# Gate and up projection from seven block products instead of eight, with the down projection as a stage of its own

## The chip, the cores and the metric

The kernel runs on one core of a Trainium2 chip. The metric is the device time of one execution in microseconds (us): the median of three runs of the kernel before is 2223.04 us (2222.63 to 2224.3). All tensors are float32; every product is made of float32r passes.

## The reference, cut to what matters

The reference is one layer of a streaming encoder on 512 tokens of width 2048: an input projection, three groups of mixing heads (attention, convolution, spatial gating), an output projection with residual, and a gated feed forward of width 5632. The change touches the feed forward and what lies around it:

```python
x = x + jnp.einsum('bse,ed->bsd', y, w_out[l])
h = rms_norm(x, ffn_norm[l])
gate = causal_depthwise_conv(jnp.einsum('bsd,df->bsf', h, w_gate[l]), ffn_conv_w[l], ffn_conv_b[l])
up = jnp.einsum('bsd,df->bsf', h, w_up[l])
x = x + jnp.einsum('bsf,fd->bsd', jax.nn.silu(gate) * up, w_down[l])
return rms_norm(x, final_norm)
```

Here h is 512 x 2048, w_gate and w_up are 2048 x 5632, the depthwise convolution has three taps along the tokens, and w_down is 5632 x 2048.

## The kernel before

The names P, S, KT, NT and NF stand for 128 partitions, 512 tokens, 16 tiles of 128 along the width, 4 token tiles and 44 tiles of 128 along the feed-forward width.

Every product is taken three times, in `mm3` (line 291): each operand is split into a part rounded to float32r and the exact rest, and hi*hi, hi*lo and lo*hi are added up in one PSUM bank. `split` (line 255) makes the two parts: ScalarE copies the operand to float32r (`w_hi`), and then VectorE subtracts that copy from the operand (`w_lo`). Both inputs of the subtraction lie in SBUF. The norm of the residual stream is applied after the product, as a scale of each token (`row2`).

The weights come in chunks of 512 KB through three buffers (`w_load`, line 246), in the order of one list, `plan`. `w_split` (line 262) splits half a chunk, that is 128 x 512 elements, and issues the next load. The matmul loops use half a chunk at a time and issue the split of the half chunk that comes two later (`w_ahead`, line 287), so that ScalarE and VectorE work ahead of TensorE.

`proj_t` (line 296) makes 256 columns of a projection, transposed: two PSUM banks of 128 columns x 512 tokens, each from 16 x 3 matmuls with a weight tile of 128 x 128 as the stationary and 512 tokens as the moving operand. `proj_n` (line 315), used earlier for other columns, makes its products with the activations as the stationary and 256 columns of weights as the moving operand; the trace names its banks `pn`.

After the output projection (lines 866 to 879) the residual stream stays in 16 SBUF tiles. Lines 880 to 883 turn it into the transposed and split operand `hT2` of the feed forward: 64 transposes on TensorE, 16 activations on ScalarE and 16 operations on VectorE (`load_transposed`, line 400). The feed forward (lines 910 to 941) runs over 11 groups of 512 columns. A group has four products of 256 columns: gate, up, gate, up. After a gate product, VectorE scales its banks, ScalarE applies the last tap and the bias, VectorE adds the two other taps, and ScalarE applies silu. After an up product, VectorE scales the bank, GpSimd multiplies it with the gate (`ff_t`), and the result is split and kept in SBUF. One column block of the down projection of the group before (`down`, line 897, banks `pd`) follows each product; VectorE adds its four banks to the residual tiles. The last group's down projection is taken token tile by token tile together with the final norm (lines 943 to 975, banks `pl`).

Each engine takes its instructions in the order in which they are issued, and the order is written out by hand: the splits of later weights stand between the matmuls of the present ones. Before the feed forward a planner (`Issue`) sets side work between the projections; in the feed forward none is left.

## Time and profile before

| What | Value |
|---|---|
| median of 3 runs | 2223.04 us (2222.63 to 2224.3) |
| the profiled execution: its span, from first to last instruction | 2222.3 us, 0.7 us less than that median |
| TensorE busy | 2188.3 us, 98% |
| VectorE busy | 1171.5 us, 53% |
| ScalarE busy | 844.5 us, 38% |
| GpSimd busy | 222.3 us, 10% |
| mean DMA rate | 96 GB/s |

The profile shows one execution. PE is TensorE, PEld its weight load, DVE is VectorE, ACT is ScalarE, POOL is GpSimd, SP is the engine that issues the DMAs (SPq is its queue). L105 is the line through which all three of ScalarE, VectorE and GpSimd are called, and L168 that of all matmuls, so that the tile names tell the groups apart: `pt` banks of a transposed projection, `pn` of a natural one, `po` of the output projection, `pd` and `pl` of the down projection. In a row of the timeline stand the start, the time from there to the end of the last merged instruction, the engine, the line, the operation, the tile written and those read, the shapes and the count; in brackets the idle time of the engine before it and what ended it. In a group of instructions stand the busy time, the mean duration of one in ns, and the idle time before them. In a table by stretch each engine's busy time and count is followed by the granted clock of TensorE (1.00 is 2.4 GHz, 0.50 is 1.2 GHz), the share of time for which the DMA engines were busy, and the rate. Matmuls are pipelined: the distance between two starts, not the duration, tells what one costs in a stream.

### The profile page before, as it was taken

How to read it: one execution, taken by the hardware profiler on the slowest of the kernel's cores; microseconds unless marked ns; L12 is line 12 of the kernel's file. 1: busy time of each engine (PE TensorE's matmuls, PEld its weight loads, DVE VectorE, ACT ScalarE, POOL GpSimd, SP SyncE). 2: the span in 40 equal slices, each digit the busy share in tenths (PEclk: the TensorE clock that was granted, in tenths of full speed). 3: DMA queues.
4: the chain of work that ended last, by engine and by line, in shares of the span. 5: the costliest groups of instructions: out<-in, count | busy, mean ns of one | idle time of the engine just before them, and what ended most of it. 6: DMA issues, size and time to landing. Idle time of an engine off the chain costs nothing.

```text
span 2222.3 us, 26797 instructions
## 1 busy us (share of the span) xinstructions
PE 2188.3 (98%) x10361; PEld 1831.2 (82%) x10361; DVE 1171.5 (53%) x1828; ACT 844.5 (38%) x1516; POOL 222.3 (10%) x295
## 2 busy tenths in 40 slices
PE   8999999999999999999999999999999999999998
PEld 7888888898788888888888888888888888888886
DVE  4789897986733444444444344344334434434446
ACT  5335567767632423222222222232222223222233
POOL 2012232322200000000000000000000000000002
PEclk9999999999999999999999999999999999999999
DMA  5332222222243232332332333233233333323343
GB/s 179 95 93 79 67 68 66 67 62 67 76 142 121 88 96 95 105 95 86 107 102 87 103 95 97 93 105 95 85 112 97 92 98 97 99 89 104 95 131 106
DMA packets 176559, 213.20 MB, mean 96 GB/s; under 512 B 6981, under 2 KB 138929, under 8 KB 176433
## 3 DMA queue, kind: packets, MB, share of 16 engines
q1 hardware_dynamic: 175873, 211.23, 30.6%
q8 instruction: 81, 1.33, 0.2%
q14 instruction: 45, 0.37, 0.1%
q10 hardware_dynamic: 560, 0.27, 0.0%
HBM read 207.28 MB, written 4.19 MB: 95 GB/s over the span
## 4 chain that ended last, share of the span: by engine, by line
PE 89%; DVE 6%; ACT 2%; issue 1%; POOL 1%; DMA 0%; SPq 0%; ACTq 0%; POOLq 0%; DVEq 0%
PE pt L168 53%; PE pd L168 20%; PE po L168 8%; PE pn L168 3%; PE pl L168 2%; DVE cv_acc L105 1%; DVE w_lo L105 1%; ACT e L105 1%; PE av L168 1%; PE ps_tr L172 1%; PE z_C L168 1%; PE z_A L168 1%; PE z_B L168 0%; DVE wt_lo L105 0%; POOL newton L105 0%
## 5 line engine op out<-in xcount | busy, mean ns | idle before, releaser
L105 DVE TENSOR_TENSOR w_lo<-w_raw,w_hi 128x512 fp32r<-128x512 f32 x752 | 521.3, 705 | 765.4 <-ACT w_hi L105 765.1
L105 ACT CAST w_hi<-w_raw 128x512 fp32r<-128x512 f32 x752 | 456.6, 621 | 928.4 <-PE pt L168 681.8
L168 PE MATMUL pt<-hT_hi,w_hi 128*128 128x512 f32 x1856 | 723.4, 390 | 0.1
L168 PE MATMUL pt<-hT_hi,w_lo 128*128 128x512 f32 x1856 | 723.2, 390 | 0.3 <-DVE w_lo L105 0.3
L168 PE MATMUL pt<-hT_lo,w_hi 128*128 128x512 f32 x1856 | 723.1, 390 | 0.0
L168 PEld LDWEIGHTS pt<-hT_hi,w_lo 128*128 128x128 f32 x1856 | 348.5, 188 | 73.8 <-DVE w_lo L105 1.2
L168 PEld LDWEIGHTS pt<-hT_hi,w_hi 128*128 128x128 f32 x1856 | 348.6, 188 | 71.3 <-ACT w_hi L105 0.8
L168 PEld LDWEIGHTS pt<-hT_lo,w_hi 128*128 128x128 f32 x1856 | 348.6, 188 | 70.2
L168 PE MATMUL pd<-w_hi,t_hi 128*128 128x512 f32 x640 | 249.0, 389 | 0.0
L168 PE MATMUL pd<-w_lo,t_hi 128*128 128x512 f32 x640 | 249.0, 389 | 0.0
L168 PE MATMUL pd<-w_hi,t_lo 128*128 128x512 f32 x640 | 249.0, 389 | 0.0
L105 POOL TENSOR_TENSOR ff_t<-ff_t,ff_c 128x512 f32<-128x512 f32 x44 | 56.8, 1290 | 1316.9 <-DVE ff_t L105 1316.9
L168 PEld LDWEIGHTS pd<-w_lo,t_hi 128*128 128x128 f32 x640 | 120.1, 188 | 25.0
L168 PEld LDWEIGHTS pd<-w_hi,t_lo 128*128 128x128 f32 x640 | 120.1, 188 | 24.9
L168 PEld LDWEIGHTS pd<-w_hi,t_hi 128*128 128x128 f32 x640 | 120.1, 188 | 24.9
L168 PE MATMUL pn<-w_hi,hT_hi 128*128 128x256 f32 x384 | 108.6, 283 | 0.0
L168 PE MATMUL pn<-w_hi,hT_lo 128*128 128x256 f32 x384 | 108.5, 283 | 0.0
L168 PE MATMUL pn<-w_lo,hT_hi 128*128 128x256 f32 x384 | 108.5, 282 | 0.0
L168 PE MATMUL po<-w_hi,yT_hi 128*128 128x512 f32 x256 | 100.5, 393 | 2.6 <-DVE sg_u L105 2.6
L168 PE MATMUL po<-w_lo,yT_hi 128*128 128x512 f32 x256 | 100.2, 391 | 0.0
L168 PE MATMUL po<-w_hi,yT_lo 128*128 128x512 f32 x256 | 100.1, 391 | 0.0
L105 DVE TENSOR_TENSOR x<-x,pd 128x512 f32<-128x512 f32 x160 | 98.9, 680 | 0.0
(212 smaller groups left out, 1998.4 us busy)
## 6 DMA issues: line engine op xcount, KB each, us to landing
w_raw<-in_w_gate_dram SPq DMA_DIRECT2D x88, 512.0 KB
w_raw<-in_w_up_dram SPq DMA_DIRECT2D x88, 512.0 KB
w_raw<-in_w_down_dram SPq DMA_DIRECT2D x88, 512.0 KB
w_raw<-in_w_in_dram SPq DMA_DIRECT2D x80, 512.0 KB
w_raw<-in_w_out_dram SPq DMA_DIRECT2D x32, 512.0 KB
x<-in_x_dram SPq DMA_DIRECT2D x32, 256.0 KB
out_dram<-x SPq DMA_DIRECT2D x16, 256.0 KB
gain<-in_final_norm_dram SPq DMA_DIRECT2D x4, 256.0 KB
```

What stands on the lines that cost most here:

```text
L105: ins = f(*a, **k)
L168: return nc.tensor.matmul(o, lhsT=lhsT, rhs=rhs, start=start, stop=stop, skip_group_check=True)
L172: nc.tensor.transpose(out=o, in_=in_, identity=identity)
```

## The change

The mathematics of gate and up changes. The 2048 rows of the weights are taken as two halves, the 256 columns of a product as two halves of 128, and the 512 tokens as two halves of 256. The eight block products of this 2 x 2 x 2 scheme are replaced by seven products of sums of blocks. On the side of the activations the seven operands (`R11`, `R21`, `R22`, `T1` to `T4`) are made once, for each of the eight pairs of width tiles, and split. On the side of the weights, four of the seven operands (`S1` to `S4`) are sums of blocks that GpSimd makes anew for each product; all seven are split as before. A product of 256 columns then has 14 units (7 block products, each in two halves of four width tiles) of 12 matmuls, with a weight tile of 128 x 128 as the stationary and 256 tokens as the moving operand. The four quarters of the result are added up by VectorE from four half banks.

The down projection is taken out of the loop over gate and up. The gated result of each tile of 128 columns is stored to a tensor in HBM (`t_dram`), and the residual stream as well (`x1_dram`); a stage behind the last product loads both again. This stage takes the down projection in four runs over ten tiles each, with all four column blocks, and the last four tiles token tile by token tile as before. SBUF is cut into pools that belong to stages: a pool of a later stage takes the room of an earlier one, tile by tile as these come free.

The diff, cut to its core:

```diff
+    groups = [(w, 256 * fp) for fp in range(NF // 2) for w in (w_gate, w_up)]
+    def blk_load(g):
+        if g < len(groups):
+            src, c0 = groups[g]
+            for h in range(2):
+                for q in range(2):
+                    t = raw_pool.tile([P, 4, 256], F32, tag="raw", bufs=6, name="b_raw")
+                    k0 = (8 * h + 4 * q) * P
+                    nc.sync.dma_start(
+                        out=t, in_=src[k0 : k0 + 4 * P, c0 : c0 + 256].rearrange("(k p) c -> p k c", p=P)
+                    )
+                    blk[g, h, q] = t
...
             add2(tt, nb, x1[nb][tt])
-    hT2 = []
+            nc.sync.dma_start(out=x1_dram[nb][tt], in_=x1[nb][tt])
+        if nb == 3:
+            blk_load(0)
...
     with tc.issue_after(end.ins):
-        for nb in range(4):
-            hT2 += load_transposed(x1[nb], nb, mm if nb % 2 == 0 else zz, 32)
+        for j in range(8):
+            fa, fb, ta, tb = (tmp(n) for n in ("f_a", "f_b", "t_a", "t_b"))
+            for kt, f in ((j, fa), (j + 8, fb)):
+                ps = zz("ps_tr")
+                for tt in range(NT):
+                    transpose(
+                        ps[:, tt * P : (tt + 1) * P], x1[kt // 4][tt][:, (kt % 4) * P : (kt % 4 + 1) * P], ident
+                    )
+                act_.activation(f, ps, AF.Copy, scale=gcol(32 + kt))
+            hi = ap.tile([P, 7, HT], F32R, name=f"R_hi{j}")
+            lo = ap.tile([P, 7, HT], F32R, name=f"R_lo{j}")
+            r11, r12, r21, r22 = fa[:, 0:HT], fa[:, HT:S], fb[:, 0:HT], fb[:, HT:S]
+            split(hi[:, 0, :], lo[:, 0, :], r11)
+            vec.tensor_tensor(out=ta[:, 0:HT], in0=r12, in1=r11, op=ALU.subtract)
+            pool.tensor_tensor(out=tb[:, 0:HT], in0=r22, in1=r12, op=ALU.subtract)
+            vec.tensor_tensor(out=ta[:, HT:S], in0=r22, in1=ta[:, 0:HT], op=ALU.subtract)
+            pool.tensor_tensor(out=tb[:, HT:S], in0=r21, in1=ta[:, HT:S], op=ALU.subtract)
+            for at, src in ((5, fb), (1, ta), (3, tb)):
+                split(
+                    hi[:, at : at + 2, :], lo[:, at : at + 2, :], src.rearrange("p (n t) -> p n t", n=2)
+                )
+            Rm.append((hi, lo))
...
+    SEQ = (
+        ("L11", "R11"), ("S1", "T1"), ("L12", "R21"), ("S3", "T3"), ("S2", "T2"), ("S4", "R22"), ("L22", "T4"),
+    )
+    UNITS = [(g, i, q) for g in range(len(groups)) for i in range(7) for q in range(2)]
+    SUMS = {
+        "S1": ("L21", "L22", ALU.add), "S3": ("L11", "L21", ALU.subtract),
+        "S2": ("S1", "L11", ALU.subtract), "S4": ("L12", "S2", ALU.subtract),
+    }
+    def make_sum(n):
...
+        if name in SUMS:
+            a, b, op = SUMS[name]
+            t = sp.tile([P, 4, P], F32, tag="sum", bufs=6, name="b_sum")
+            pool.tensor_tensor(out=t, in0=operand(g, a, q), in1=operand(g, b, q), op=op)
+            sums[g, name, q] = t
+    def make_split(n):
...
+        if i == 0 and q == 0:
+            blk_load(g + 1)
+        hi = sp.tile([P, 4, P], F32R, tag="bhi", bufs=5, name="b_hi")
+        lo = sp.tile([P, 4, P], F32R, tag="blo", bufs=5, name="b_lo")
+        split(hi, lo, operand(g, SEQ[i][0], q))
+        parts[n] = (hi, lo)
...
+    def gate_out(f, c):
+        vec.tensor_tensor(out=c, in0=c, in1=row2, op=ALU.mult)
+        s = tmp("ff_c")
+        act_.activation(s, c, AF.Identity, bias=fcol(3, f), scale=fcol(2, f))
+        for k in (1, 0):
+            sh = 2 - k
+            vec.scalar_tensor_tensor(
+                out=s[:, sh:S], in0=c[:, 0 : S - sh], scalar=fcol(k, f), in1=s[:, sh:S],
+                op0=ALU.mult, op1=ALU.add,
+            )
+        act_.activation(s, s, AF.Silu)
+        pool.tensor_tensor(out=s, in0=s, in1=row2, op=ALU.mult)
+        sil[f] = s
+    def up_out(f, c):
+        pool.tensor_tensor(out=c, in0=c, in1=sil.pop(f), op=ALU.mult)
+        nc.sync.dma_start(out=t_dram[f], in_=c)
+    AHEAD, SUM_AHEAD = 4, 6
...
+        b1, b2 = mm("pt"), mm("pt")
+        X, Y, Z1, Z2 = b1[:, 0:HT], b1[:, HT:S], b2[:, 0:HT], b2[:, HT:S]
+        acc = {0: X, 1: Z1, 2: Y, 3: Z2, 4: X, 5: Z1, 6: Z2}
+        c0, c1 = tmp("ff_g0"), tmp("ff_g1")
+        for i in range(7):
+            for q in range(2):
+                make_sum(n + SUM_AHEAD)
+                make_split(n + AHEAD)
+                hi, lo = parts.pop(n)
+                at = R_AT[SEQ[i][1]]
+                for kk in range(4):
+                    rh, rl = Rm[4 * q + kk]
+                    mm3(
+                        acc[i], hi[:, kk, :], lo[:, kk, :], rh[:, at, :], rl[:, at, :],
+                        i < 2 and q == 0 and kk == 0, q == 1 and kk == 3,
+                    )
+                n += 1
+            if i == 2:
+                vec.tensor_copy(c0[:, 0:HT], X)
+                vec.tensor_tensor(out=c0[:, 0:HT], in0=c0[:, 0:HT], in1=Y, op=ALU.add)
+            elif i == 3:
+                vec.tensor_copy(c1[:, HT:S], Z1)
+                vec.tensor_tensor(out=c1[:, HT:S], in0=c1[:, HT:S], in1=Z2, op=ALU.add)
+            elif i == 4:
+                u = tmp("ff_u")[:, 0:HT]
+                act_.copy(u, X)
+                vec.tensor_tensor(out=c1[:, HT:S], in0=c1[:, HT:S], in1=u, op=ALU.add)
+            elif i == 5:
+                vec.tensor_tensor(out=c0[:, HT:S], in0=u, in1=Z1, op=ALU.add)
+                out_fn(f0, c0)
+            elif i == 6:
+                vec.tensor_tensor(out=c1[:, 0:HT], in0=u, in1=Z2, op=ALU.add)
+                out_fn(f0 + 1, c1)
...
+    for f in range(4):
+        t_load(f)
+        dn_load(f)
+    t_next = 0
+    for _ in range(4):
+        t_split(t_next)
+        t_next += 1
+    for j in range(3):
+        dn_split(j)
...
+    for kg in range(4):
+        for nb in range(4):
+            banks = [(mm if nb % 2 else zz)("pd") for _ in range(NT)]
+            if kg == 0:
+                for tt in range(NT):
+                    nc.sync.dma_start(out=x1[nb][tt], in_=x1_dram[nb][tt])
+            for f in range(10 * kg, 10 * kg + 10):
+                if t_next < min(NF, 10 * kg + 24) and (t_next < 10 * kg + 10 or j % 2 == 0):
+                    t_split(t_next)
+                    t_next += 1
...
+                for tt in range(NT):
+                    ts_ = slice(tt * P, (tt + 1) * P)
+                    th, tl = t_parts[f]
+                    mm3(banks[tt], th[:, ts_], tl[:, ts_], hi, lo, f == 10 * kg, f == 10 * kg + 9)
+            for tt in range(NT):
+                vec.tensor_tensor(out=x1[nb][tt], in0=x1[nb][tt], in1=banks[tt], op=ALU.add)
```

`raw_block` takes 128 of the 256 columns of a loaded chunk, and `operand` takes such a block or a sum. `t_split` and `dn_split` split a tile of the gated result and half a chunk of `w_down`.

## Rows read from the trace of the kernel before

**Rows 1.** The page: busy time of each engine.
```profile
PE 2188.3 (98%) x10361; PEld 1831.2 (82%) x10361; DVE 1171.5 (53%) x1828; ACT 844.5 (38%) x1516; POOL 222.3 (10%) x295
```
**Rows 2.** The chain of waits in order: start us, us, what.
```profile
928.52 21.76 PE pt L168 x96
950.28 10.88 PE pd L168 x48
```
**Rows 3.** Timeline of TensorE: first and nineteenth matmul of a stretch of `proj_n`.
```profile
111.76 0.28 PE L168 MATMUL pn<-w_hi,hT_hi 128*128 128x256 f32 x1
...
113.92 0.28 PE L168 MATMUL pn<-w_hi,hT_hi 128*128 128x256 f32 x1
```
**Rows 4.** Groups of instructions by form in the feed forward, 790 to 2165 us.
```profile
L105 DVE TENSOR_TENSOR w_lo<-w_raw,w_hi 128x512 fp32r<-128x512 f32 x508 | 342.9, 690 | 615.3 <-ACT w_hi L105 615.3
L105 DVE SCALAR_TENSOR_TENSOR ff_c<-ff_g,cols_f,ff_c 128x511 f32<-128x511 f32 x44 | 33.1, 751 | 38.0 <-ACT ff_c L105 38.0
L105 ACT CAST w_hi<-w_raw 128x512 fp32r<-128x512 f32 x507 | 306.4, 622 | 709.5 <-PE pt L168 596.6 <-PE pd L168 110.8 <-DMA w_raw<-in_w_down_dram 2.2
L105 ACT ACTIVATE ff_c<-ff_g,cols_f 128x512 f32<-128x512 f32 x44 | 35.6, 808 | 52.1 <-DVE ff_g L105 52.1
L105 ACT ACTIVATE ff_c<-ff_c 128x512 f32<-128x512 f32 x44 | 27.8, 633 | 71.6 <-DVE ff_c L105 71.6
L105 POOL TENSOR_TENSOR ff_t<-ff_t,ff_c 128x512 f32<-128x512 f32 x44 | 56.8, 1290 | 1316.9 <-DVE ff_t L105 1316.9
```
**Rows 5.** Timeline of VectorE: two `w_lo` without GpSimd, at 779 us.
```profile
779.53 1.28 DVE L105 TENSOR_TENSOR w_lo<-w_raw,w_hi 128x512 fp32r<-128x512 f32 x2
```
**Rows 6.** Timeline of VectorE beside GpSimd, 113 to 121 us.
```profile
117.44 3.48 DVE L105 TENSOR_TENSOR w_lo<-w_raw,w_hi 128x512 fp32r<-128x512 f32 x2
120.85 0.73 DVE L105 SCALAR_TENSOR_TENSOR cv_acc<-cv_a,cols_c,cv_acc 128x507 f32<-128x507 f32 x1
```
**Rows 7.** Timeline of GpSimd in the same stretch.
```profile
115.23 3.44 POOL L105 TENSOR_TENSOR cv_a<-cv_a,cv_g 128x512 f32<-128x512 f32 x2
118.64 1.74 POOL L105 TENSOR_TENSOR cv_acc<-cv_acc,cv_sq 128x512 f32<-128x512 f32 x1
```
**Rows 8.** Timeline of VectorE beside GpSimd, with an operand in PSUM.
```profile
366.29 1.27 DVE L105 TENSOR_TENSOR k_f<-pt,row_x 128x512 f32<-128x512 f32 x2
367.49 0.67 DVE L105 TENSOR_TENSOR w_lo<-w_raw,w_hi 128x512 fp32r<-128x512 f32 x1
```
**Rows 9.** Timeline of GpSimd in that stretch.
```profile
365.87 1.66 POOL L105 TENSOR_TENSOR sq<-sq,newton 128x512 f32<-128x512 f32 x1
```
**Rows 10.** Groups by form: 256 columns on VectorE and on ScalarE.
```profile
L105 DVE TENSOR_TENSOR v<-vf,v 128x256 fp32r<-128x256 f32 x16 | 6.7, 419 | 1.9 <-ACT v L105 1.8
L105 ACT CAST v<-vf 128x256 fp32r<-128x256 f32 x16 | 6.5, 407 | 0.5
```
**Rows 11.** Timeline of TensorE and ScalarE between output projection and feed forward.
```profile
765.25 8.74 PE L172 MATMUL ps_tr<-ident,x 128*128 128x128 f32 x64
774.00 0.50 PE L168 MATMUL pt<-hT_hi,w_hi 128*128 128x512 f32 x1
...
767.22 9.35 ACT L105 ACTIVATE hT_hi<-ps_tr,cols_a 128x512 fp32r<-128x512 f32 x16
```
**Rows 12.** Table by stretch: the first 20 us, and around 450 us.
```profile
0.00:10.00 10.00, 4.30 (x16) 3.34 (x17) 1.45 (x3) 3.06 (x4) 4.37 (x22) 1.00 0.76 244
10.00:20.00 10.00, 9.75 (x46) 7.88 (x46) 7.04 (x11) 8.97 (x22) 0.73 (x4) 1.00 0.95 336
445.00:449.80 4.80, 3.15 (x14) 2.02 (x13) 4.73 (x7) 0.60 (x1) 2.72 (x4) 1.00 0.30 91
449.80:453.30 3.50, 3.50 (x13) 2.94 (x13) 2.81 (x5) 2.38 (x5) 0.00 (x0) 0.51 0.09 29
```
**Rows 13.** Timeline of TensorE at the lower clock, 591 to 593 us.
```profile
590.88 0.63 PE L168 MATMUL po<-w_hi,yT_lo 128*128 128x512 f32 x1
...
592.58 0.63 PE L168 MATMUL po<-w_hi,yT_hi 128*128 128x512 f32 x1
```

More of the change, by code (lines that the diff above doesn't have):

```diff
@@ L944, in trunk_kernel @@
-    gain = [s2k("gain") for _ in range(4)]
+    t_dram = [dram.tile([P, S], F32, name=f"t_{f}") for f in range(NF)]
+    sil = {}
+    def gate_out(f, c):
[11 more added lines that the diff above has]
+        sil[f] = s
@@ new lines, in up_out @@
+    def up_out(f, c):
+        pool.tensor_tensor(out=c, in0=c, in1=sil.pop(f), op=ALU.mult)
+        nc.sync.dma_start(out=t_dram[f], in_=c)
+    AHEAD, SUM_AHEAD = 4, 6
+    for n in range(SUM_AHEAD):
+        make_sum(n)
+        if n < AHEAD:
+            make_split(n)
+    n = 0
+    for g in range(len(groups)):
+        f0 = 2 * (g // 2)
+        out_fn = gate_out if g % 2 == 0 else up_out
+        b1, b2 = mm("pt"), mm("pt")
[31 more added lines that the diff above has]
+                out_fn(f0 + 1, c1)
@@ new lines, in trunk_kernel, with dn_load @@
+    a_stage.close()
+    up_stage.close()
+    d_stage = ctx.enter_context(ExitStack())
+    dp = d_stage.enter_context(tc.tile_pool(name="down", bufs=1, reuse_waits="tile"))
+    dplan = [(f, nb) for kg in range(4) for nb in range(4) for f in range(10 * kg, 10 * kg + 10, 2)]
+    dplan += [(f, nb) for nb in range(4) for f in (40, 42)]
+    n_steps = 2 * 16 * 5
+    raw_d, halves_d, t_parts = {}, {}, {}
+    def dn_load(i):
+        if i < len(dplan):
+            f, nb = dplan[i]
+            raw_d[i] = dp.tile([P, 2, S], F32, tag="raw", bufs=4, name="w_raw")
+            nc.sync.dma_start(
+                out=raw_d[i],
+                in_=w_down[f * P : (f + 2) * P, nb * S : (nb + 1) * S].rearrange("(k p) c -> p k c", p=P),
+            )
@@ new lines, in big, with dn_split @@
+    def big(name):
+        return dp.tile([P, S], F32R, tag="big", bufs=52, name=name)
+    def dn_split(j):
+        i, s = divmod(j, 2)
+        if i >= len(dplan):
+            return
+        if j < n_steps:
+            hi = dp.tile([P, S], F32R, tag="whi", bufs=4, name="w_hi")
+            lo = dp.tile([P, S], F32R, tag="wlo", bufs=4, name="w_lo")
+        else:
+            hi, lo = big("w_hi"), big("w_lo")
+        split(hi, lo, raw_d[i][:, s, :])
+        halves_d[j] = (hi, lo)
+        if s == 1:
+            del raw_d[i]
+            dn_load(i + 4)
@@ new lines, in trunk_kernel, with t_load, t_split @@
+    t_raw = {}
+    def t_load(f):
+        if f < NF:
+            t_raw[f] = dp.tile([P, S], F32, tag="t_raw", bufs=4, name="t_raw")
+            nc.sync.dma_start(out=t_raw[f], in_=t_dram[f])
+    def t_split(f):
+        if f < NF:
+            hi, lo = big("t_hi"), big("t_lo")
+            split(hi, lo, t_raw.pop(f))
+            t_parts[f] = (hi, lo)
+            t_load(f + 4)
+    for f in range(4):
[5 more added lines that the diff above has]
+        t_next += 1
```

146 lines of the change are left out of this document (67 added, 79 removed).

## The prediction

> **What bounds the kernel now.** I read the page's first part and then the chain of waits. TensorE is busy for 98% of the span, VectorE for 53%, GpSimd for 10% [rows 1]. The chain, followed through the feed forward, is TensorE alone: a gate or up product of 96 matmuls takes 21.76 us, a block of the down projection 10.88 us, one behind the other with nothing between them [rows 2]. So a matmul of 512 columns costs 21.76/96 = 0.2267 us in a stream, and the 44 products 957.4 us. VectorE waits here: its `w_lo` group has 343 us of work and 615 us of idle time ahead of it, waiting for ScalarE [rows 4], and ScalarE's copies in their turn wait for TensorE to free a buffer. The change takes work from TensorE, the bound, and gives work to the engines that have time left. The question is how much time these really have when they run together.
>
> **TensorE's share.** A product has 14 units of 12 matmuls, 168 in all, each with 256 moving columns behind a weight tile of 128 x 128. That shape is in the trace: `proj_n` starts nineteen of them between 111.76 and 113.92 us, 18 steps in 2.16 us, 0.120 us each [rows 3]. Half of 0.2267 would be 0.113, so 0.006 us per matmul goes to the smaller size. A product then takes 168 x 0.120 = 20.1 us instead of 21.76, a pair of gate and up 40.2 instead of 43.5, and the 22 pairs 884 instead of 957. That is 73 us, and it is all that the change can bring. The down projection keeps its 1920 + 192 matmuls at the old price.
>
> **What the other engines have to do per pair.** From `SEQ`, `SUMS`, `gate_out` and `up_out` I count for one gate and one up product:
> - VectorE, both inputs in SBUF, 512 wide: 28 `lo` splits (14 units each), 2 scalings by `row2`, 4 taps. That is 34, at 0.69 to 0.75 us alone [rows 4]; two directly behind each other take 1.28 us [rows 5], so 0.60 us each in a stream.
> - VectorE, both inputs in SBUF, 256 wide: 2 additions of `u`, 0.42 us [rows 10].
> - VectorE with an operand in PSUM, 256 wide: 12. No row shows one; I bound them by 0 (hidden, see below) and the 0.42 us of rows 10.
> - ScalarE: 28 copies at 0.62, 2 at 0.41 [rows 10], 2 first taps at 0.81 and 2 silu at 0.63 [rows 4]: 21 us, within any of the times below.
> - GpSimd, both inputs in SBUF, 512 wide: 16 sums, 2 scalings and 2 products. That is 20, at 1.29 us each [rows 4], 25.8 us.
>
> Each engine alone would fit into 40.2 us: VectorE with 34 x 0.69 + 0.8 + 12 x 0.42 = 29.3, GpSimd with 25.8. Together they don't. Between 115 and 121 us both have such work queued, and they take turns: GpSimd's multiplications start at 115.23 and, two of them later, at 118.64, VectorE's `w_lo` at 117.44 and, two later, 120.85 us [rows 6, 7]. That is 3.41 us for two of each, 1.70 us for one of each. A `w_lo` that takes 0.60 alone lasts 1.74 beside GpSimd. So every GpSimd operation that meets a waiting VectorE costs VectorE 1.70 - 0.60 = 1.10 us. What escapes this is an operation with one input in PSUM: two `k_f` from `pt` take 1.27 us, their usual time, inside a GpSimd multiplication that runs from 365.87 to 367.53 us [rows 8, 9]. In the feed forward before, GpSimd had 44 operations in 1375 us [rows 4], so nothing of this shows in its rows.
>
> The Trainium skill has this as a rule (SBUF — State Buffer, "Who interferes with whom"): a VectorE instruction with two SBUF inputs and a GpSimd instruction that reads SBUF exclude each other for the whole instruction, and one with at most one SBUF input does not contend. The trace agrees on who contends, and puts the pair at 1.70 us where whole durations would add up to 1.29 + 0.69 = 1.98. By whole durations the 34, 2 and 20 operations would take 23.5 + 0.8 + 25.8 = 50.1 us per pair and the kernel 2410 us, inside my range; I keep the measured 1.70.
>
> **The price of a pair.** Below: only what excludes each other, everything else hidden beneath it: 34 x 0.60 + 2 x 0.42 + 20 x 1.10 = 20.4 + 0.8 + 22.0 = 43.2 us. Above: nothing hidden. Then VectorE's 34 operations stand alone with 0.69, the PSUM operations add 5.0, and in `gate_out` VectorE waits for the first tap (0.81) and, since ScalarE takes silu (0.63) ahead of the next `hi` copy (0.62), for these two as well, twice per pair: 4.1. Sum 23.5 + 0.8 + 22.0 + 5.0 + 4.1 = 55.4 us. The end below is 3 us more than TensorE needs, so VectorE's queue, held up by GpSimd, becomes the bound. GpSimd has its sums queued six units ahead and can run them while VectorE reads PSUM or waits, which is what rows 8 and 9 show; so I take the third nearer the lower end, 47.5 us. The 22 pairs then take 1045 us against 957.4: **+87.6 us**. The four units of splits ahead (5.7 us of TensorE work) even out single waits, not a queue that is too long on average.
>
> **Before the first product.** Now TensorE transposes for 8.74 us from 765.25, and the first matmul follows at 774.00, while ScalarE still works on the operand from 767.22 [rows 11]. After, the first split of a weight stands behind all eight steps `j` in the queues. Per step ScalarE has two scalings, three copies of 512 and one of 256. In a stream of 16 a 512-wide one takes 9.35/16 = 0.58 us: 5 x 0.58 + 0.35 = 3.25. With the durations of a lone one (0.69, 0.62, 0.41) it is 3.7, and the last copy of a step waits for GpSimd's second difference, which waits for VectorE's: about 1 us more. So 26 to 37 us from 767.2, then one split (0.62 + 0.69): TensorE starts at 794.5 to 805.5 instead of 774.0. I take **+27 us**, above the middle, because the waits stand in the step's own chain. GpSimd's sums stand behind `tb` only, and the first weight blocks land in this time. The 16 stores of the residual wait for nobody's result.
>
> **Between the last product and the down stage.** The room of its buffers comes free with the last matmuls, and SP is held by the last store, which waits for an addition (0.42) and a GpSimd product (1.29). Then SP issues `t` and `w_down` loads in turn, and ScalarE takes four `t` tiles before the first weight: 4 x 256 + 3 x 512 KB = 2.6 MB ahead. At the 244 to 336 GB/s of the first 20 us [rows 12] that is 8 to 11 us, then two copies and a subtraction (1.9): 9 (if the store doesn't hold SP) to 15 us of TensorE time. **+12 us**, where before there was no gap.
>
> **What costs nothing.** A unit's loads: 2 MB per product in 20 us or more, as before. The third and fourth block of the next product wait for GpSimd's last sums, and the stores of `up_out` are queued on SP behind them; only a `tmp` buffer used ten tiles later waits for these. If that cover goes, it is the landing of 512 KB, 2 us at the rates above, per product. In the down stage the reloads bring a block of 27.2 us to 6.9 MB at most, 254 GB/s, in the first of four runs; if they were late, 244 GB/s instead would cost 1 us per block, 4 us. VectorE saves 96 additions, which were hidden.
>
> **The clock.** The two gaps idle TensorE. After a stretch with 3.15 of 4.80 us busy the granted clock was 0.51, the 1.2 GHz level, for 3.5 us [rows 12], and matmuls of 512 stood (592.58 - 590.88)/4 = 0.425 us apart [rows 13]: 8 of them instead of 15, 1.6 to 1.8 us lost each time. Two gaps: **+3.6 us**. In the feed forward the waits after `gate_out` could do the same, at most 22 x 1.7 = 37 us; I count none, since they come in pieces.
>
> **Sum**: 2222.3 + 87.6 + 27 + 12 + 3.6 = 2352.5, and 0.7 for the distance of the profiled execution to the median: 2353 us.
>
> **Rivals.**
> - TensorE stays the bound, because GpSimd's operations fall into VectorE's pauses: pairs of 40.2 us. For it: each engine alone fits. Against it: the operations that exclude each other need 43.2. Time 2222.3 - 957.4 + 884 + 42.6 + 0.7 = 2192 us, faster. The point from which it decides: the kernel is faster with pairs under (957.4 - 42.6)/22 = 41.6 us, that is where a GpSimd operation costs VectorE under 1.02 us (20.4 + 0.8 + 20 x 1.02). 13%.
> - The pair at its floor, 43.2 to 45.5 us: 2259 to 2309 us. For it: GpSimd beside PSUM reads [rows 8, 9]. Against it: the waits in `gate_out`. 18%.
> - Little is hidden, pairs of 50.5 to 55.4 us, or the clock falls with every pair: above 2419, up to 2527 us. For it: the waits on ScalarE's chain, as the 38 us before `ff_c` [rows 4]. 16%.
>
> **How the numbers follow.** My forecast is pairs of 45.5 to 50.5 us, 2309 to 2419 us, 50%. Pairs between 40.9 and 43.2 us, 2208 to 2259, get the remaining 3%, which fall on both sides. A measurement of this kernel can tell a change of 0.2%, 4 us: faster 14%, within 1%, slower 85%. The range of 2220 to 2465 leaves out the fast rival and the top of the slow one.
>
> **What would show it.** `pt` matmuls still 0.120 us apart inside a unit, but TensorE waiting for `b_lo` of VectorE between units; `b_lo` near 1.1 us on the mean instead of 0.69, GpSimd's `b_sum` above 1.29; about 47 us from one gate product to the next; the first `pt` near 801 us; some 12 us without matmuls ahead of `pd`, whose blocks stay at 0.2267 us per matmul. Wrong would be: `b_lo` at 0.69 beside busy GpSimd, or TensorE without waits in the feed forward.

## The result, and the profile after

| | before | after |
|---|---|---|
| median (lowest to highest of 4 runs) | 2222.90 us (2222.63 to 2224.30) | 2370.15 us (2369.55 to 2372.41) |
| span of the profiled execution | 2222.3 us | 2368.3 us |
| ratio, 95% interval | | 1.0663 (1.0648 to 1.0678) |

The change makes the kernel 6.6% slower. The forecast was 2353 us; the time lies within its range (2220 to 2465 us) and its likeliest case (2309 to 2419 us).

Five stretches account for the 146.0 us. They run between starts of matmuls: up to the first `pt` of the feed forward; from there to the last `pt`; to the first `pd`; to the first `pl`; and to the end. For before, the stretch from the first `pt` to the first `pl` is 1394.7 us; less 40 blocks of the down projection at 10.88 [rows 2], 959.5 us are left for gate and up.

| stretch | before | after | difference | forecast |
|---|---|---|---|---|
| first `pt` starts at | 774.0 | 809.2 | +35.2 | +27 |
| gate and up, 22 pairs | 959.5 | 1054.0 | +94.5 | +87.6 |
| last `pt` to first `pd` | 0 | 14.4 | +14.4 | +12 |
| down projection to the first `pl` | 435.2 | 437.6 | +2.4 | in the +3.6 for the clock |
| end | 53.6 | 53.1 | -0.5 | 0 |

The page's first part, after: TensorE is busy a little longer than before although it has fewer products to make, and VectorE and GpSimd are busy for 572 and 663 us more [rows 1]. An operation that is held up counts as busy for its whole duration.

```profile
PE 2201.1 (93%) x13529; PEld 1982.0 (84%) x13529; DVE 1743.5 (74%) x2292; ACT 1028.4 (43%) x1856; POOL 885.2 (37%) x707
```

The matmuls themselves are as forecast [rows 3]. On the timeline of TensorE inside a unit they start 0.120 us apart:

```profile
1519.83 0.28 PE L172 MATMUL pt<-R_lo,b_hi 128*128 128x256 f32 x1
1519.95 0.28 PE L172 MATMUL pt<-R_hi,b_lo 128*128 128x256 f32 x1
1520.07 0.28 PE L172 MATMUL pt<-R_hi,b_hi 128*128 128x256 f32 x1
```

But a pair of products takes 47.82 us (median of the distances between gate activations), not 40.3. In the groups by form of the feed forward, 810 to 1864 us, against [rows 4], a `lo` split lasts 1.14 to 1.28 us instead of 0.69, a GpSimd sum 1.49 to 1.74 instead of 1.29, and TensorE waits in the main for `b_hi` and `b_lo`:

```profile
L172 PE MATMUL pt<-R_hi,b_hi 128*128 128x256 f32 x2463 | 726.1, 295 | 64.7 <-ACT b_hi L105 51.3 <-DVE ff_g L105 13.4
L172 PE MATMUL pt<-R_hi,b_lo 128*128 128x256 f32 x2464 | 717.3, 294 | 24.6 <-DVE b_lo L105 24.6
...
L105 DVE TENSOR_TENSOR b_lo<-b_sum,b_hi 128x512 fp32r<-128x512 f32 x352 | 437.1, 1275 | 22.6 <-ACT b_hi L105 19.5
L105 DVE TENSOR_TENSOR b_lo<-b_raw,b_hi 128x512 fp32r<-128x512 f32 x263 | 292.3, 1144 | 29.3 <-ACT b_hi L105 28.7
L105 POOL TENSOR_TENSOR b_sum<-b_raw 128x512 f32<-128x512 f32 x172 | 290.4, 1717 | 66.1 <-DVE b_lo L105 66.1
...
L105 POOL TENSOR_TENSOR b_sum<-b_sum,b_raw 128x512 f32<-128x512 f32 x86 | 148.1, 1742 | 0.0
L105 POOL TENSOR_TENSOR b_sum<-b_raw,b_sum 128x512 f32<-128x512 f32 x88 | 130.3, 1491 | 48.2 <-DVE b_lo L105 47.2 <-DVE ff_g L105 1.0
```

In the table by stretch, one pair is cut in two (busy time and count of TensorE, its weight loads, VectorE, ScalarE, GpSimd; then granted clock, DMA share, rate):

```profile
1511.40:1545.00 33.60, 33.60 (x259) 33.48 (x260) 32.23 (x35) 14.21 (x25) 25.94 (x16) 0.92 0.26 85
1545.00:1559.35 14.35, 10.69 (x79) 9.68 (x78) 11.94 (x15) 5.78 (x10) 6.15 (x4) 0.94 0.42 133
```

In the first 33.6 us TensorE never pauses, and VectorE is busy for 32.2 of them. All of TensorE's pauses of this pair fall into the last 14.35 us, where the gate's result is finished. The timeline there, of VectorE, ScalarE, GpSimd, and the matmuls that waited:

```profile
1547.37 0.82 ACT L105 ACTIVATE ff_c<-ff_g,cols_f 128x512 f32<-128x512 f32 x1 [2.68 <-DVE ff_g L105]
...
1548.22 1.54 DVE L105 SCALAR_TENSOR_TENSOR ff_c<-ff_g,cols_f,ff_c 128x511 f32<-128x511 f32 x2 [0.89 <-ACT ff_c L105]
...
1552.84 3.29 POOL L105 TENSOR_TENSOR b_sum<-b_raw,b_sum 128x512 f32<-128x512 f32 x2 [0.69 <-DVE b_lo L105]
...
1553.22 3.46 DVE L105 SCALAR_TENSOR_TENSOR ff_c<-ff_g,cols_f,ff_c 128x511 f32<-128x511 f32 x2
...
1556.77 0.63 ACT L105 ACTIVATE ff_c<-ff_c 128x512 f32<-128x512 f32 x1 [4.53 <-DVE ff_c L105]
1557.30 1.12 ACT L105 CAST b_hi<-b_raw 128x512 fp32r<-128x512 f32 x2
...
1557.96 0.58 PE L172 MATMUL pt<-R_hi,b_hi 128*128 128x256 f32 x1 [2.32 <-ACT b_hi L105]
...
1559.35 0.58 PE L172 MATMUL pt<-R_hi,b_lo 128*128 128x256 f32 x1 [0.60 <-DVE b_lo L105]
```

VectorE's two taps of the pair's first gate tile (1548.22) take 1.54 us, those of the second (1553.22) 3.46, because two sums on GpSimd run from 1552.84. ScalarE waits 4.53 us for them with its silu, and the next two `b_hi` copies stand behind that silu in its queue, so TensorE waits 2.32 us. In this pause the clock falls to the 1.2 GHz level; the table by stretch has it right behind the pause, and back at 2.4 GHz six microseconds later:

```profile
1558.30:1563.30 5.00, 4.40 (x20) 4.11 (x20) 5.00 (x6) 2.30 (x5) 3.17 (x3) 0.50 0.00 0
1564.60:1569.60 5.00, 5.00 (x44) 5.00 (x43) 4.87 (x8) 2.16 (x4) 5.00 (x4) 1.00 0.00 0
```

The clock records of the trace have 18 such stretches that begin in the feed forward, 119.5 us in all. Its 1054.0 us divide into 7392 matmuls x 0.120 = 887.0, pauses of 116.2 (gaps of over 0.3 us between starts, less 0.120 each), and 50.8 that remain for matmuls at the lower clock.

### The profile page after: what moved, and what is told of

The parts are those of the page before. It is cut to its first block, busy times and chain, and to the rows that moved or that the text cites. A ratio compares the mean times of both kernels' runs of the same rounds, so it can differ in the third digit from the quotient of the medians.

```text
span 2368.3 us, 35579 instructions
## 1 busy us (share of the span) xinstructions
PE 2201.1 (93%) x13529; PEld 1982.0 (84%) x13529; DVE 1743.5 (74%) x2292; ACT 1028.4 (43%) x1856; POOL 885.2 (37%) x707
## 3 DMA queue, kind: packets, MB, share of 16 engines
q8 instruction: 106, 1.74, 0.3%
## 4 chain that ended last, share of the span: by engine, by line
PE 70%; DVE 17%; ACT 5%; issue 4%; POOL 2%; DMA 1%; SPq 0%; ACTq 0%; DVEq 0%; POOLq 0%
PE pt L172 38%; PE pd L172 18%; PE po L172 7%; DVE b_lo L105 5%; DVE ff_c L105 5%; PE pn L172 3%; PE pl L172 2%; DVE ff_g L105 2%; DVE cv_acc L105 1%; DVE w_lo L105 1%; ACT b_hi L105 1%; ACT ff_c L105 1%; ACT e L105 1%; PE av L172 1%; PE z_C L172 1%
## 5 line engine op out<-in xcount | busy, mean ns | idle before, releaser
L172 PE MATMUL pt<-R_hi,b_hi 128*128 128x256 f32 x2464 | 726.7, 295 | 69.2 <-ACT b_hi L105 55.7
L172 PE MATMUL pt<-R_hi,b_lo 128*128 128x256 f32 x2464 | 717.3, 294 | 24.6 <-DVE b_lo L105 24.6
L172 PE MATMUL pt<-R_lo,b_hi 128*128 128x256 f32 x2464 | 716.6, 291 | 0.0
L172 PEld LDWEIGHTS pt<-R_hi,b_hi 128*128 128x128 f32 x2464 | 494.2, 201 | 82.3 <-ACT b_hi L105 67.6
L172 PEld LDWEIGHTS pt<-R_hi,b_lo 128*128 128x128 f32 x2464 | 489.1, 200 | 37.6 <-DVE b_lo L105 35.5
L172 PEld LDWEIGHTS pt<-R_lo,b_hi 128*128 128x128 f32 x2464 | 494.5, 201 | 0.0
L105 DVE TENSOR_TENSOR b_lo<-b_sum,b_hi 128x512 fp32r<-128x512 f32 x352 | 437.1, 1275 | 22.6 <-ACT b_hi L105 19.5
L172 PE MATMUL pt<-hT_hi,w_hi 128*128 128x512 f32 x448 | 175.5, 392 | 0.2
L172 PE MATMUL pt<-hT_hi,w_lo 128*128 128x512 f32 x448 | 175.2, 391 | 0.3 <-DVE w_lo L105 0.3
L172 PE MATMUL pt<-hT_lo,w_hi 128*128 128x512 f32 x448 | 175.0, 391 | 0.0
L172 PEld LDWEIGHTS pd<-w_hi,t_hi 128*128 128x128 f32 x640 | 120.7, 189 | 39.5 <-ACT w_hi L105 14.3
```

The costliest lines, as they stand in the source:

```text
L105: ins = f(*a, **k)
L172: return nc.tensor.matmul(o, lhsT=lhsT, rhs=rhs, start=start, stop=stop, skip_group_check=True)
```

## The experiments

Theory 1 is the prediction's main term: VectorE and GpSimd hold each other up. Theory 2: the cost is the chain VectorE, ScalarE, VectorE, ScalarE behind a gate product (scaling, first tap, two taps, silu). One execution each unless an interval is given; the four of the changed kernel lie within 3 us of one another. "Pair" is the median as above, "VectorE per pair" is its busy time between 900 and 1600 us, divided by 700, times the pair, and "at half clock" counts the stretches that begin in the feed forward.

| kernel | time, us | pair | VectorE per pair | pauses | at half clock |
|---|---|---|---|---|---|
| after | 2370.15 | 47.82 | 44.3 | 116.2 | 119.5 |
| e1_no_sums | 2262.24 | 43.13 | 31.1 | 50.6 | 0 |
| e2_no_chain | 2318.13 | 45.75 | 41.3 | 80.9 | 47.7 |
| e3_spread | 2309.39 | 44.82 | 41.1 | 85.6 | 17.1 |
| e4_row_in_R | 2310.47 | 44.75 | 39.1 | 74.7 | 27.3 |
| e5_vec_sums | 2298.59 | 44.10 | 40.0 | 76.1 | 37.5 |
| e6_spread_no_sums | 2207.68 | 40.67 | 30.1 | 1.6 | 0 |
| e9_half_sums | 2304.81 | 45.12 | 41.4 | 81.5 | 37.5 |
| e11_fill | 2356.24 | 47.12 | 42.3 | 84.2 (131.7 less 22 x 18 x 0.120 of fillers) | 13.6 |
| e8_all | 2203.48 | 40.77 | 34.8 | 3.6 | 0 |

The rows behind the fourth column, from the tables by stretch (the third busy time is VectorE's). The kernel after:

```profile
900.00:1600.00 700.00, 642.88 (x4957) 626.25 (x4956) 647.98 (x705) 293.78 (x500) 468.63 (x293) 0.95 0.32 102
```

Sums left out:

```profile
900.00:1600.00 700.00, 672.66 (x5458) 658.89 (x5457) 504.13 (x780) 323.99 (x551) 103.56 (x64) 1.00 0.35 111
```

Steps of the gate spread:

```profile
900.00:1600.00 700.00, 651.13 (x5224) 636.91 (x5225) 641.43 (x745) 314.76 (x527) 501.93 (x311) 0.99 0.34 107
```

Sums on VectorE:

```profile
900.00:1600.00 700.00, 655.41 (x5242) 643.72 (x5241) 634.31 (x999) 312.58 (x532) 93.89 (x62) 0.98 0.34 106
```

Sums left out and steps spread:

```profile
900.00:1600.00 700.00, 700.00 (x5785) 695.73 (x5784) 517.81 (x828) 353.70 (x586) 114.41 (x68) 1.00 0.38 117
```

The version with both taken out and nothing left out:

```profile
900.00:1600.00 700.00, 699.90 (x5768) 694.43 (x5767) 597.98 (x1028) 362.82 (x652) 0.00 (x0) 1.00 0.37 117
```

**e1_no_sums**: GpSimd's 16 sums per pair are left out; raw blocks stand in for them.

```diff
+            sums[g, name, q] = raw_block(g, {"S1": "L21", "S3": "L11", "S2": "L22", "S4": "L12"}[name], q)
+        elif name in SUMS:
```

> The changed kernel with GpSimd's 16 sums per pair left out: the four sum operands are replaced by plain weight blocks, so the products of sums are left out of the computation. Same matmuls, splits and order otherwise. Theory 1, the shared way into SBUF: VectorE loses no time to GpSimd, has a reserve of over 10 us per pair, and evens out what follows a gate product; pairs of gate and up at 40.2 to 41.5 us, the 1.2 GHz stretches gone, b_lo at about 0.70 us, total 2205 to 2235 us. Theory 2, the chain between VectorE and ScalarE in gate_out (scaling, first tap, two taps, silu, next copy): that chain is untouched, so TensorE still stands some 4 us per pair and the clock falls; pairs at 45 to 47 us, total 2310 to 2355 us.

Measured: pairs of 43.13 and 2262.24 us, between the ranges of the two theories, and no stretch at half clock. The sums cost 4.7 us of the 47.8. But 2.8 us over TensorE's 40.3 stay although VectorE is busy for only 31.1. In the waits of TensorE between 900 and 1600 us (total, times, longest) they are behind `b_lo` and `b_hi`:

```profile
PE pt L172 <- DVE b_lo L105: 21.2, 32, 0.9
PE pt L172 <- ACT b_hi L105: 6.2, 16, 0.4
```

**e2_no_chain**: the first tap reads `row2`, the other two write into `c`, so that nothing waits for anything between the engines; the convolution is left out by that.

```diff
-        act_.activation(s, c, AF.Identity, bias=fcol(3, f), scale=fcol(2, f))
+        act_.activation(s, row2, AF.Identity, bias=fcol(3, f), scale=fcol(2, f))
-                out=s[:, sh:S], in0=c[:, 0 : S - sh], scalar=fcol(k, f), in1=s[:, sh:S],
+                out=c[:, sh:S], in0=row2[:, 0 : S - sh], scalar=fcol(k, f), in1=c[:, sh:S],
```

> The changed kernel with the same instructions on every engine in gate_out, but the first tap reads the token scales instead of the scaled gate, and the two other taps are written over the scaled gate, so that VectorE and ScalarE don't wait for each other there; the convolution is left out of the computation by that. GpSimd's 20 operations per pair stay. Theory 1: VectorE and GpSimd still exclude each other for 43.2 us per pair, so pairs at 43.5 to 46.5 us, total 2280 to 2345 us, b_lo still near 1.2 us. Theory 2: the waits are gone, pairs at 40.2 to 41.5 us, no 1.2 GHz stretches, total 2205 to 2235 us although b_lo stays near 1.2 us.

**e3_spread**: the same instructions, but the four steps behind a gate product are issued one per unit of 12 matmuls, each behind that unit's split.

```diff
+        vec.tensor_tensor(out=c, in0=c, in1=row2, op=ALU.mult)
+        later.extend((
+            lambda: act_.activation(s, c, AF.Identity, bias=fcol(3, f), scale=fcol(2, f)),
+            lambda: tap(1), lambda: tap(0), silu,
+        ))
...
+                if later:
+                    later.pop(0)()
```

> The changed kernel with gate_out spread: the scaling at once, then first tap, second tap, third tap, silu with its product, one of them after the split of each following unit, so that four splits stand between the waits. All instructions and results as in the changed kernel. Theory 1: VectorE's queue is as long as before, pairs at 43.5 to 46.5 us, total 2280 to 2345 us. Theory 2: the waits are covered by the splits ahead, pairs at 40.2 to 42 us, hardly a 1.2 GHz stretch, total 2205 to 2245 us.

**e4_row_in_R**: the token scale goes into the seven operands, so that the scalings by `row2` (two on VectorE, two on GpSimd per pair) are gone from the feed forward.

```diff
-                act_.activation(f, ps, AF.Copy, scale=gcol(32 + kt))
+                vec.scalar_tensor_tensor(
+                    out=f, in0=ps, scalar=gcol(32 + kt), in1=row2, op0=ALU.mult, op1=ALU.mult
+                )
...
-        vec.tensor_tensor(out=c, in0=c, in1=row2, op=ALU.mult)
-        pool.tensor_tensor(out=s, in0=s, in1=row2, op=ALU.mult)
```

> The changed kernel with the token scales put into the activations' operands once, ahead of the feed forward (VectorE instead of ScalarE evacuates the transposes, times gain times scale), so that per pair VectorE has 2 and GpSimd 2 operations of 512 less; the order in gate_out stays. Theory 1: 34 becomes 32, 20 becomes 18, floor 19.2 + 0.8 + 19.8 = 39.8 us; pairs at 41 to 44.5 us. Theory 2: the chain is shorter by the scaling alone (0.69 us and what GpSimd holds it up), pairs at 45.5 to 47.3 us. Ahead of the first product 5 to 12 us more under both (token scales first, 16 operations more on VectorE). Totals: theory 1 2225 to 2310, theory 2 2320 to 2370 us.

Measured in these three: pairs of 45.75, 44.82 and 44.75. The times of e2 and e3 lie in the ranges of theory 1; that of e4 is 0.5 us above the range given for theory 1 there. Each takes 2 to 3 us from a pair, none comes to the 40.3 of TensorE, and with the sums in place VectorE stays busy for 39.1 to 41.3 us. In e3_spread TensorE's idle time hardly stands behind ScalarE's `b_hi` any more (4.4 us in the feed forward, 51.3 in the changed kernel) but behind VectorE: its reads of the half banks (`ff_g`, 42.8) and `b_lo` (24.0). Theory 2 alone is refuted, and so is theory 1 alone by e1.

**e5_vec_sums**: the sums are made, but by VectorE.

```diff
-            pool.tensor_tensor(out=t, in0=operand(g, a, q), in1=operand(g, b, q), op=op)
+            vec.tensor_tensor(out=t, in0=operand(g, a, q), in1=operand(g, b, q), op=op)
```

> The 16 sums of a pair move from GpSimd to VectorE; GpSimd keeps the 4 products with the gate. Theory 1 (VectorE and GpSimd hold each other up): VectorE has 16 more instructions a pair, but each runs at its own 0.60 to 0.69 us and only four of GpSimd's stand in its way: 50 x 0.60 + 0.84 + 4.6 + 4 x 1.1 = 39.8 us a pair, under TensorE's 40.2. The pairs then go by TensorE and the gate chain alone, 42 to 44 us (43.1 where the sums were left out), b_lo falls from 1218 ns to 800 or less, and the time is 2245 to 2290 us, faster than the changed kernel although VectorE does more. Theory 2 (only the chain between VectorE and ScalarE at the end of a pair costs): the chain is the same and VectorE has more queued ahead of it, so pairs stay at 47 us or more and the time is 2350 us or more.

Measured: 2298.59 us, 8.6 over the range of theory 1, with pairs of 44.10 (42 to 44 expected), but on its side: VectorE is busy for 40.0 us per pair (39.8 expected), 4.3 less than with the sums on GpSimd, while it executes 16 instructions more. This is the price in one number: a sum costs VectorE (40.0 - 31.1)/16 = 0.56 us when it makes it, and (44.3 - 31.1)/16 = 0.83 us when GpSimd makes it (0.69 between e3_spread and e6_spread_no_sums). The Trainium skill (SBUF — State Buffer, "Who interferes with whom") says that the two exclude each other for the whole instruction. Who contends agrees with the rows. The price of a sum is not the 1.29 us of a whole GpSimd operation, though: 0.69 to 0.83 was lost.

**e6_spread_no_sums**: e1 and e3 together; the sums are again left out.

> Both causes are out: GpSimd's 16 sums a pair are left out of the computation (blocks stand in for them), and the steps of the gate at the end of a pair are spread one to a unit. If port and chain are the whole of what a pair has over TensorE's own rate, pairs take 40.2 to 41.0 us, idle time of TensorE in the feed forward falls under 15 us with no half-clock stretch, and the time is 2200 to 2225 us. If there is a third cause, pairs stay above 42 us and the time above 2240 us.

Measured: pairs of 40.67, pauses of 1.6 us in all, the clock at 1.00. GpSimd's sums (the "port" of the expectation) and the chain together are the whole of a pair's excess, within the 0.4 us that are left over TensorE's 40.3. With e1 and e3 this makes four kernels, with both causes, without each and without both, and they price them: the sums cost 4.7 us of a pair beside the chain (47.82 - 43.13) and 4.2 without it (44.82 - 40.67), the chain 3.0 beside the sums and 2.5 without them. The two nearly add up to the 7.2 us.

**e9_half_sums**: e3_spread with `S1` and `S3` on VectorE.

```diff
-            pool.tensor_tensor(out=t, in0=operand(g, a, q), in1=operand(g, b, q), op=op)
+            (vec if name in ("S1", "S3") else pool).tensor_tensor(out=t, in0=operand(g, a, q), in1=operand(g, b, q), op=op)
```

> The kernel with the spread gate steps, and of its 16 sums a pair 8 (S1 and S3) on VectorE and 8 (S2 and S4) on GpSimd. With all on GpSimd a pair took 44.8 us, with the sums left out 40.7. If VectorE's time is what counts, its own instructions and a price for each of GpSimd's, then 34 x 0.60 + 0.84 + 4.6 + 20 x p = 44.8 gives p = 0.95 us, and with half moved a pair takes 42 x 0.60 + 0.84 + 4.6 + 12 x 0.95 = 42.0 us: FFN about 927 us, time about 2245 us. If it counts only how late single operands are, not the sum, pairs are at 40.7 (TensorE hides it) or still at 44 and more.

Measured: pairs of 45.12, no better than with all 16 on GpSimd (44.82), and VectorE no less busy (41.4). The time, 2304.81 us, is 4.6 lower than that of e3_spread only because the first product starts earlier (802.4 us, 810.9 in e3_spread). My calculation by a fixed price failed. In the groups of GpSimd (900 to 1600 us) its sums now wait 231 of 700 us for VectorE (168 in e3_spread), and what ends the wait is a split (`b_lo`), not a sum that VectorE makes:

```profile
L105 POOL TENSOR_TENSOR b_sum<-b_raw,b_sum 128x512 f32<-128x512 f32 x63 | 88.1, 1398 | 113.3 <-DVE b_lo L105 81.5 <-issue 20.5 <-POOL b_sum L105 11.3
L105 POOL TENSOR_TENSOR b_sum<-b_sum,b_raw 128x512 f32<-128x512 f32 x62 | 79.7, 1285 | 149.9 <-DVE b_lo L105 149.9
```

So VectorE's queue holds GpSimd up as well. Why that takes back the whole saving is not shown, and whether another choice of eight sums would do better was not tried.

**e11_fill**: 18 matmuls more per pair, where TensorE idles longest; their result is read by nobody.

```diff
+                if g % 2 == 1 and i == 2 and q == 0:
+                    fill = zz("fill")
+                    for _ in range(18):
+                        nc.tensor.matmul(
+                            fill[:, 0:HT], lhsT=Rm[0][0][:, 0, 0:P], rhs=Rm[0][0][:, 0, :],
+                            start=True, stop=True, skip_group_check=True,
+                        )
```

> The changed kernel with 18 products of TensorE more in every pair (18 x 0.120 = 2.2 us, on operands that are long there, into a bank that nobody reads), put where it idles longest (2.6 us, ahead of the fifth block of the second half of the pair). If the half-clock stretches follow from that idle time, they go (119.5 us at half clock to under 20), pairs take 47.8 - 50.8 / 22 = 45.5 us, and the time is about 2320 us although TensorE computes more. If the clock falls for another reason, the stretches stay, pairs are at 47.8 us or above, and the time is 2370 us or more.

Measured: the half-clock time falls from 119.5 to 13.6 us, as expected: it follows from the pause. But the pair goes from 47.82 to 47.12 only, not to 45.5, and the kernel from 2370 to 2356 us, not to 2320. The table by stretch for the whole feed forward, after and then this kernel:

```profile
809.97:1864.50 1054.53, 964.21 (x7390) 938.51 (x7390) 964.93 (x1055) 439.16 (x747) 694.24 (x434) 0.94 0.30 96
```
```profile
810.80:1849.50 1038.70, 975.02 (x7743) 942.63 (x7741) 926.57 (x1055) 438.67 (x746) 700.38 (x433) 0.99 0.31 98
```

At full clock TensorE merely comes to its next wait sooner. The 50.8 us that the lower clock seemed to take were worth some 16 (1054.0 - 1038.1), as far as the fillers themselves delayed nothing. The changed kernel's own trace shows the same without fillers. All its 22 pairs have the pause of 2.3 us, but behind four of them the clock stayed at 2.4 GHz. There TensorE waits once more, 1.55 us for VectorE, as in these lines of its timeline; the next long pause comes 47.44 us after the first:

```profile
984.70 0.39 PE L172 MATMUL pt<-R_hi,b_hi 128*128 128x256 f32 x1 [2.31 <-ACT b_hi L105]
...
993.41 0.36 PE L172 MATMUL pt<-R_hi,b_hi 128*128 128x256 f32 x1 [1.55 <-DVE ff_g L105]
...
1032.14 0.58 PE L172 MATMUL pt<-R_hi,b_hi 128*128 128x256 f32 x1 [2.33 <-ACT b_hi L105]
```

Where the clock fell for 6.8 us behind the pause, the next one comes after 47.8 to 47.95 us (16 distances). A stretch at half clock thus cost the pair about 0.4 us, with nothing changed in the kernel: what sets the pair is VectorE's queue with the gate's chain, not TensorE.

**e7_edges**: GpSimd's order is kept as written from the token steps to the last product, and the first splits of the down stage stand in the order of use.

```diff
+    iss.keep.add("gpsimd")
...
+    iss.keep.discard("gpsimd")
...
-    for _ in range(4):
-        t_split(t_next)
-        t_next += 1
-    for j in range(3):
-        dn_split(j)
+    t_split(0)
+    dn_split(0)
+    dn_split(1)
+    t_split(1)
+    dn_split(2)
...
```

> Only the edges: GpSimd's instructions are kept in the order of the program, so that its sums for later steps no longer stand ahead of the copies of the last token steps, and the first splits of the down stage are put in the order in which the products want them. If the order of GpSimd's queue made the front longer than forecast, the stretch from the last attention product to the first product of the feed forward goes from 45.7 to about 36 us, the stretch before the down stage from 14.4 to about 8 us, pairs stay at 47.8 us, and the time is about 2354 us. If the front waits for something else (the DMA of the blocks, ScalarE's copies), it stays at 44 us or more and the time at 2362 us or more.

Measured: 2439.74 us, a miss by 86. The stretch before the down stage falls from 14.4 to 8.7 us as expected, the front (from the last `po` matmul of the output projection to the first `pt`) from 45.7 to 41.7 only, and the pairs rise to 51.24. The timeline of GpSimd shows why: eight sums in one block, then the gate's products in their written place, where GpSimd waits 5.68 and 2.35 us with the next sums behind them:

```profile
1506.99 3.43 POOL L106 TENSOR_TENSOR b_sum<-b_raw 128x512 f32<-128x512 f32 x2
...
1517.12 3.40 POOL L106 TENSOR_TENSOR b_sum<-b_raw 128x512 f32<-128x512 f32 x2
1526.20 1.29 POOL L106 TENSOR_TENSOR ff_g<-ff_g,ff_c 128x512 f32<-128x512 f32 x1 [5.68 <-DVE ff_g L106]
1529.85 1.29 POOL L106 TENSOR_TENSOR ff_g<-ff_g,ff_c 128x512 f32<-128x512 f32 x1 [2.35 <-ACT b_hi L106]
1531.11 1.74 POOL L106 TENSOR_TENSOR b_sum<-b_raw 128x512 f32<-128x512 f32 x1
```

From 1531.11 on ScalarE waits for every sum (its timeline), and the splits run at GpSimd's pace of 1.70 us where TensorE takes 1.44 per unit:

```profile
1534.58 0.63 ACT L106 CAST b_hi<-b_sum 128x512 fp32r<-128x512 f32 x1 [1.08 <-POOL b_sum L106]
1536.29 0.62 ACT L106 CAST b_hi<-b_sum 128x512 fp32r<-128x512 f32 x1 [1.08 <-POOL b_sum L106]
```

**e10_front_only**: as e7, but the order is given free again behind the token steps.

```diff
     row2 = token_row(rstd2, "x1")
+    iss.keep.discard("gpsimd")
```

> As the kernel with reordered edges, but GpSimd is kept in the order of the program only while the seven operands of the tokens are built. If it was the kept order in the feed forward that took its pairs from 47.8 to 51.2 us (the products of the gate behind the sums), pairs are back at 47.8 us; the front stays at 41.7 and the stretch before the down stage at 8.7 us, and the time is about 2360 us. If the pairs stay over 50 us, something else in that kernel made them long, and the time is over 2430 us.

Measured: 2363.09 us; pairs back at 47.80, which confirms the cause of e7's miss, and 8.6 before `pd`. The front, though, is 49.4, not 41.7: sums, whose order is free here, stand ahead of the last token steps again, and the first `pt` waits behind the row of token scales, for which TensorE waits until GpSimd has made `diag` (timelines of GpSimd and TensorE):

```profile
786.39 6.45 POOL L106 TENSOR_TENSOR b_sum<-b_raw 128x512 f32<-128x512 f32 x4
792.80 2.84 POOL L106 TENSOR_TENSOR b_sum<-b_sum,b_raw 128x512 f32<-128x512 f32 x2
795.61 1.16 POOL L106 TENSOR_TENSOR t_b<-f_b,f_a 128x256 f32<-128x256 f32 x1
```
```profile
809.27 2.55 PE L173 MATMUL ps_row<-diag,ones_f 128*128 128x128 f32 x8 [23.47 <-POOL diag L106]
811.47 0.56 PE L173 MATMUL pt<-R_hi,b_hi 128*128 128x256 f32 x1
```

**e8_all**: a version made from these findings, with the seven products. All sums and all products of the feed forward and the differences of the token steps on VectorE, GpSimd without work there; no `row2` (the transposes multiply by a diagonal of the token scales) and each step's transposes issued a step ahead; the copies of `X` and `Z1` on ScalarE; gate steps spread; written order kept on VectorE and GpSimd; first splits of the down stage in the order of use.

```diff
-            pool.tensor_tensor(out=t, in0=operand(g, a, q), in1=operand(g, b, q), op=op)
+            vec.tensor_tensor(out=t, in0=operand(g, a, q), in1=operand(g, b, q), op=op)
...
-        pool.tensor_tensor(out=c, in0=c, in1=sil.pop(f), op=ALU.mult)
+        vec.tensor_tensor(out=c, in0=c, in1=sil.pop(f), op=ALU.mult)
...
-                vec.tensor_copy(c0[:, 0:HT], X)
+                act_.copy(c0[:, 0:HT], X)
...
+                matmul(
+                    ps[:, tt * P : (tt + 1) * P], x1[kt // 4][tt][:, (kt % 4) * P : (kt % 4 + 1) * P],
+                    dgs[tt], True, True, f32=True,
+                )
```

> Seven products kept, with both causes taken out without leaving anything out of the computation: all sums and gate products on VectorE, GpSimd idle in the feed forward, token scales folded in ahead of the feed forward, gate steps spread, edges put in order. By port and chain together a pair falls to TensorE's own 40.2 to 41.5 us, the front to about 35 us, the stretch before the down stage to about 8 us: about 2185 to 2215 us, under the 2222.6 us of the kernel before. If VectorE with 54 sums and products a pair is too full (54 x 0.60 + 0.84 + 4.6 = 37.8 us of 40.2), pairs stay at 43 us or more and the time is 2250 us or more.

Measured: 2203.48 us (2202.42 to 2204.84, 4 runs) against 2223.53 for before on the same chip; ratio 0.9911 (0.9894 to 0.9927). It is 0.9% faster than the kernel before. VectorE has 50 operations of 512 per pair, not the 54 of the expectation: the scalings by `row2` are gone, and two products have come. Its busy time is 34.8 us. In its groups by form a `lo` split takes the 0.69 us that it takes alone, and a sum on VectorE 0.68:

```profile
L106 DVE TENSOR_TENSOR b_lo<-b_sum,b_hi 128x512 fp32r<-128x512 f32 x349 | 237.5, 686 | 71.4 <-ACT b_hi L106 70.9
...
L106 DVE TENSOR_TENSOR b_lo<-b_raw,b_hi 128x512 fp32r<-128x512 f32 x260 | 178.4, 686 | 14.6 <-ACT b_hi L106 10.1
...
L106 DVE TENSOR_TENSOR b_sum<-b_raw 128x512 f32<-128x512 f32 x172 | 117.7, 684 | 0.0
```

Pairs of 40.77 save 57.5 us (959.5 - 902.0). The later first `pt` (800.3, +26.3), the stretch before `pd` (8.0) and 1.7 elsewhere take back 36.0, which leaves the 21.5 between the spans (2222.3 and 2200.8).

## Why the prediction was right, step by step

- **TensorE's share: right.** 0.120 us per matmul; with both causes out, pairs of 40.67 for 40.2 forecast (336 x 0.120 is 40.3, so the saving is 70 us, not 73).
- **The price of a pair: 47.5 forecast, 47.82 measured, and the bound is the one named.** The terms were off in both directions. VectorE's 44.3 us are 21.2 for its own work with SBUF inputs (as forecast), 12 x 0.414 = 5.0 for the operations with an operand in PSUM, which I had let lie anywhere between hidden and 5.0, and 18.1 that remain for 20 operations of GpSimd: 0.90 each, not 1.10. In the other 3.5 us VectorE waits: 0.9 for the first tap and 1.3 for the copy behind silu, so 2.2 in the gate's chain, of the 4.1 that stood in the upper bound, and 1.4 in short waits that were not in the sum. The way up, 4.3 us, was a guess by a third, and that it came out at 4.6 is luck in part: 5.0, 2.2 and 1.4 us came on top, and 3.9 went off for GpSimd, which I had priced too dear. This division also does not say what each cause would give back: spreading the chain (e3_spread) took 3.0 us from the pair, but out of VectorE's busy time (44.3 to 41.1); its waits stayed at 3.7.
- **Where TensorE waits: wrong.** I expected waits for `b_lo` between units all along, "in pieces", and counted no falls of the clock. They stand together in the last 14 us of a pair, the longest 2.3 us, more of them behind ScalarE's `b_hi` (51.3 us) than behind `b_lo` (24.6), and the clock falls 18 times. The term set at nothing was worth some 7 us by the pairs without a fall (17 x 0.4; the first fall, of 3.4 us, cost nothing) and some 16 by e11_fill, within the bound of 37 that I gave.
- **Before the first product: mis-sized, +35.2 for +27.** The step that failed is "GpSimd's sums stand behind `tb` only". They stand so in the program, but the order of GpSimd and VectorE isn't kept as written (only ScalarE's is): six sums were issued ahead of the last two token steps, and ScalarE and TensorE waited for that. These are GpSimd's and TensorE's timelines of after:

```profile
790.80 0.84 POOL L105 TENSOR_TENSOR t_b<-f_b,t_a 128x256 f32<-128x256 f32 x1 [0.36 <-DVE t_a L105]
791.60 6.45 POOL L105 TENSOR_TENSOR b_sum<-b_raw 128x512 f32<-128x512 f32 x4
798.01 1.44 POOL L105 TENSOR_TENSOR b_sum<-b_sum,b_raw 128x512 f32<-128x512 f32 x1
...
800.47 1.69 POOL L105 TENSOR_TENSOR b_sum<-b_sum,b_raw 128x512 f32<-128x512 f32 x1
802.11 0.72 POOL L105 TENSOR_TENSOR t_b<-f_b,f_a 128x256 f32<-128x256 f32 x1
```
```profile
809.16 0.58 PE L172 MATMUL pt<-R_hi,b_hi 128*128 128x256 f32 x1 [4.45 <-ACT b_hi L105]
```

  The kernels in which GpSimd makes no sums show the price: in e1_no_sums, e5_vec_sums and e6_spread_no_sums the front is 39.0 to 39.5 us instead of 45.7, and the first `pt` starts at 800.6 to 803.3, near the 801 forecast. With the sums on GpSimd and its order kept (e7_edges) the front is 4.0 us shorter, and TensorE then waits for the row of token scales; without that row (e8_all) the first `pt` is at 800.3.
- **Before the down stage: 14.4 for 12, mechanism right.** SP issues the first load at 1865.8 us, behind the store that waits for GpSimd's last product (to 1865.3), and ScalarE copies the first weight at 1876.95, behind four `t` tiles. The part that the order of the splits sets is 5.7 us (e7).
- **The fast rival** (pairs of 40.2) needed a GpSimd operation to cost VectorE under 1.02 us. It cost 0.69 to 0.90, and the pairs were still at 47.8: that condition was worked out from the lower bound, without the operations on PSUM and without the chain. A point of decision has to be taken from the whole sum.
